# Layer 1's down projection as seven Strassen products in two passes, with the sums of weights and activations on GpSimd

## The chip, the cores and the metric

The kernel runs on one core of one Trainium2 chip. The metric is device microseconds (us) of one execution. The profile names the engines PE (TensorE matmul), PEld (TensorE weight load), DVE (VectorE), ACT (ScalarE), POOL (GpSimd) and SP (SyncE, which here only issues DMAs).

## The reference

A two-layer encoder trunk over 1024 tokens of 1024 channels, float32. The change concerns the feed-forward part, whose hidden width is 2816 = 22 x 128:

```python
def swiglu_ffn(h, w_gate, w_up, w_down):
    return (jax.nn.silu(h @ w_gate) * (h @ w_up)) @ w_down

for layer in range(2):
    h = rmsnorm(x, norm_mix_g[layer])
    x = x + mixer[layer](h)        # FNet and convolution heads in layer 0, pooling in layer 1
    h = rmsnorm(x, norm_ffn_g[layer])
    x = x + swiglu_ffn(h, ffn_w_gate[layer], ffn_w_up[layer], ffn_w_down[layer])
return rmsnorm(x, final_g)
```

## The kernel before

All activations lie transposed: 128 channels on the partitions, tokens along the free axis. Every float32 product is three matmuls of the reduced type fp32r, on operands split into a high and a low part: `mm3` issues high x high (L100), high x low (L101) and low x high (L102) into one PSUM bank. `split` makes the parts: a cast on ACT (L87), then a subtraction on DVE (L88).

**Gate and up.** Both matrices go through Winograd's form of Strassen's seven products. One step p covers two chunks of 128 hidden channels; the contraction is split into two halves of the channels (four chunks of 128 each) and the tokens into two halves of 512. `gate_up_first` does the two products that need only the first token half, for p = 0 to 10, and stores their sums in DRAM. `gate_up_all` then runs the other five, as 22 units (p, gate), (p, up): S2·T2, S3·T3, S1·T1, A22·T4, S4·B22, each 12 matmuls of 128x128 by 128x512. Two pairs share a bank: A22·T4 is accumulated on S3·T3's bank and S4·B22 on S1·T1's. So A22·T4 cannot start before DVE has read S3·T3 out of its bank (L668, `u3 = bd + u2`).

`prep` makes the left operands of the unit after the one in hand: two weight tiles `raw` (128x1024, issued by SP at L590) are loaded, DVE forms four sums from them (L634, L635, L636, L643), and five splits follow. `raw` has three buffers, the split weights ten. All engines work in order, so where such an instruction stands in its engine's queue decides what waits behind it. The products of gate and up, `g` (L652), leave by three DMAs for each p on POOL's queue (L653).

**Down.** `down` goes over the tokens in two parts (the second cut into blocks of 256 in its last stage) and over three groups of 8, 7 and 7 hidden chunks. Weights and activations are both loaded by SP into `raw` and split. Each result is added to x (L726). `final`, the last norm, runs over the last 256 tokens after the last product.

A tile scheduler places the instructions of each engine in its queue; reuse of a buffer waits for its last reader. `big` has 28 buffers (x, activations and the transformed activations), `half` six, `ln` four (`s3`, `u2`), `cvp` four (`g`), `cv` and `pr` two each.

Of the kernel before, what the change touches and what calls it, by code (L numbers as in the profile page):

```python
# [42 lines left out]
def trunk(ctx: ExitStack, tc: tile.TileContext, xT, vecs, cw, w_in, w_out, fmap, pmap,  # L43
          wg, wu, wd, cen_m, pcnt, dft_h, dft_l, seq_h, seq_l, out):
    nc = tc.nc
# [100 lines left out]

# [273 lines left out]
    for h in range(4):  # L420
        w = in_w(h)
        at = big("at")
        for t in range(2):
            TT(out=at[:, HALVES[t]], in0=in_mm(w, t), in1=invs[t], op=ALU.mult)
# [87 lines left out]

# [95 lines left out]
    def gate_up_first(layer, p, bt):  # L608
        """The products that need no more than the first half of the tokens."""
        g = half("g11")  # L610
        for i, wsrc in enumerate((wg, wu)):
# [10 lines left out]
            else:  # L622
                TT(out=g, in0=ps, in1=g, op=ALU.mult)
        nc.gpsimd.dma_start(a_dram[layer][2 * p][:, HALVES[0]], g)

    def prep(layer, p, wsrc, first):
        """Left operands of the products of one matrix, in the order of their use."""
        a11, a12 = raw_w(wsrc[layer, 2 * p])
        a21, a22 = raw_w(wsrc[layer, 2 * p + 1])
# [4 lines left out]
        TT(out=s3, in0=a11, in1=a21, op=ALU.subtract)  # L634
        TT(out=a21, in0=a21, in1=a22, op=ALU.add)  # L635
        TT(out=a11, in0=a21, in1=a11, op=ALU.subtract)  # L636
        w["S2"] = opnd(a11, wt)
        w["S3"] = opnd(s3, wt)
        w["S1"] = opnd(a21, wt)
        if first:  # L640
            w["A12"] = opnd(a12, wt)
        w["A22"] = opnd(a22, wt)
        TT(out=a12, in0=a12, in1=a11, op=ALU.subtract)  # L643
        w["S4"] = opnd(a12, wt)
        return w

    def fin(layer, up, dst, src, m, t, tmp=None):
        """dst becomes silu of the gate, then the product with up, which leaves."""
        if not up:
            nc.scalar.activation(dst, src, AF.Silu)  # L650
        else:
            TT(out=dst, in0=src, in1=dst, op=ALU.mult)  # L652
            nc.gpsimd.dma_start(a_dram[layer][m][:, HALVES[t]], dst)  # L653

# [116 lines left out]

# [18 lines left out]

# [81 lines left out]

# [3 lines left out]
    def final(pi, blocks):
        for lo, hi in blocks:
            inv = norm(lo, hi)
            yield 6.0
            for k in range(KD):  # L880
                o = half("o")[:, :hi - lo]
                STT(out=o, in0=xs[k][:, lo:hi], scalar=gneg[:, V_FIN + k:V_FIN + k + 1], in1=inv,
                    op0=ALU.mult, op1=ALU.mult)
                (nc.sync if k % 2 else nc.scalar).dma_start(out[k][:, lo:hi], o)
                yield 0.65
# [91 lines left out]
```

## Time and profile before

| | |
|---|---|
| time, median of 3 runs (range) | 1742.57 us (1741.8 to 1743.17) |
| span of the profiled execution | 1740.6 us, about 2 us under the median; the runs' times take in some 2 us around the span |
| granted TensorE clock, mean | 0.99 |
| gate and up of layer 0, 22 units of five products | about 454 to 754 us |
| gate and up of layer 1, the same | about 1181 to 1479 us |
| down of layer 1 | about 1479.7 to 1729.8 us |
| last norm after the last product | about 1729.8 to 1740.6 us |

In a row of a group the columns are: line, engine, operation, tiles out<-in, shapes, count | busy us, mean ns of one | idle time ahead and what ended it. In a row of the timeline: start, length, engine, line, operation, and in brackets the idle time before it and its releaser.

### The profile page before, as it was taken

To read this page: it belongs to the slowest core of one execution; us is meant where nothing else is said; L and a number is where in the kernel's file an instruction comes from. 1 tells how busy PE (TensorE), PEld (TensorE's weight loads), DVE (VectorE), ACT (ScalarE), POOL (GpSimd) and SP (SyncE) were. 2 spreads that over 40 slices of the span, in tenths; PEclk is the share of its full clock that TensorE was granted. 3 is DMA by queue.
4 is the path that set the end of the run, shared out by engine and by line. 5 is a ranking of instruction groups with operands and counts; after the bars stand their busy time and mean duration, and the time that the engine had idled before them with its cause. 6 is when DMAs were issued, how large, how long until landed. Compare 5 with 4: busy or idle time off the path is not lost.

```text
span 1740.6 us, 22375 instructions
## 1 busy us (share of the span) xinstructions
PE 1682.0 (97%) x8318; PEld 1400.9 (80%) x8318; DVE 1245.9 (72%) x1774; ACT 692.9 (40%) x1062; POOL 276.0 (16%) x300
## 2 busy tenths in 40 slices
PE   6998899999999999999999998999999999999997
PEld 4786777777888888889998886778888888788997
DVE  8699988794577777755559768787777775545546
ACT  5455855464323232233234344553232322334223
POOL 4587764111000000000000001110000000000000
PEclk9999899999999999999999999999999999999999
DMA  5121311545633333355433425646333333644433
GB/s 188 47 97 37 135 61 46 184 142 201 232 131 122 127 109 127 116 167 174 133 109 126 152 85 182 211 163 218 133 122 127 109 127 121 204 144 160 167 122 123
DMA packets 82236, 238.66 MB, mean 137 GB/s; under 512 B 10320, under 2 KB 15696, under 8 KB 82128
## 3 DMA queue, kind: packets, MB, share of 16 engines
q1 hardware_dynamic: 65520, 186.64, 32.6%
q0 software_dynamic: 14304, 47.46, 7.2%
q10 hardware_dynamic: 2304, 3.15, 0.5%
q8 instruction: 65, 1.06, 0.3%
q14 instruction: 43, 0.35, 0.1%
HBM read 190.02 MB, written 47.19 MB: 136 GB/s over the span
## 4 chain that ended last, share of the span: by engine, by line
PE 83%; DVE 11%; DMA 3%; ACT 1%; issue 1%; SPq 0%; DVEq 0%; ACTq 0%
PE ps L100 18%; PE ps L102 18%; PE ps L101 18%; PE lnp L100 10%; PE lnp L102 10%; PE lnp L101 9%; DVE acc L313 2%; DVE acc L134 1%; DMA xin<-in_xT 1%; DMA raw<-in_wd 1%; DVE hl L88 1%; DMA raw<-in_wu 1%; DVE wl L88 1%; DVE ybl L88 0%; PE lnp L538 0%
## 5 line engine op out<-in xcount | busy, mean ns | idle before, releaser
L87 ACT CAST hl<-raw 128x512 fp32r<-128x512 f32 x264 | 161.2, 621 | 426.0 <-DVE raw L636 161.4
L100 PE MATMUL ps<-hl 128*128 128x512 f32 x704 | 277.6, 395 | 3.3 <-ACT s L617 2.8
L102 PE MATMUL ps<-hl 128*128 128x512 f32 x704 | 276.6, 393 | 0.0
L101 PE MATMUL ps<-hl 128*128 128x512 f32 x704 | 276.5, 393 | 0.0
L87 ACT CAST wh<-raw 128x896 fp32r<-128x896 f32 (+2 forms) x139 | 132.5, 953 | 243.5 <-PE ps L101 109.0
L100 PE MATMUL ps<-ahl,wh 128*128 128x256 f32 (+3 forms) x711 | 228.0, 321 | 0.5 <-ACT wh L87 0.5
L102 PE MATMUL ps<-ahl,wl 128*128 128x256 f32 (+3 forms) x711 | 227.7, 320 | 0.5 <-DVE wl L88 0.5
L101 PE MATMUL ps<-ahl,wh 128*128 128x256 f32 (+3 forms) x711 | 227.2, 320 | 0.0
L88 DVE TENSOR_TENSOR hl<-raw,hl 128x512 fp32r<-128x512 f32 x264 | 179.8, 689 | 47.9 <-ACT hl L87 43.3
L100 PE MATMUL lnp<-hl 128*128 128x512 f32 x528 | 210.2, 398 | 0.7 <-ACT s L617 0.7
L102 PE MATMUL lnp<-hl 128*128 128x512 f32 x528 | 208.1, 395 | 0.0
L101 PE MATMUL lnp<-hl 128*128 128x512 f32 x528 | 207.9, 394 | 0.0
L88 DVE TENSOR_TENSOR wl<-raw,wh 128x896 fp32r<-128x896 f32 (+2 forms) x127 | 141.6, 1116 | 48.7 <-ACT wh L87 44.3
L100 PEld LDWEIGHTS ps<-hl 128*128 128x128 f32 x704 | 132.2, 188 | 37.7 <-ACT s L617 6.9
L102 PEld LDWEIGHTS ps<-hl 128*128 128x128 f32 x704 | 132.3, 188 | 30.6
L101 PEld LDWEIGHTS ps<-hl 128*128 128x128 f32 x704 | 132.4, 188 | 29.6
L303 POOL TENSOR_TENSOR cvp<-cvp,pr 128x512 f32<-128x512 f32 x96 | 139.3, 1452 | 82.5 <-ACT pr L302 78.2
L100 PEld LDWEIGHTS ps<-ahl,wh 128*128 128x128 f32 x711 | 134.3, 189 | 11.1 <-ACT wh L87 0.9
L102 PEld LDWEIGHTS ps<-ahl,wl 128*128 128x128 f32 x711 | 134.0, 189 | 10.9 <-DVE wl L88 1.0
L101 PEld LDWEIGHTS ps<-ahl,wh 128*128 128x128 f32 x711 | 134.3, 189 | 10.2 <-issue 0.2
L653 POOL DMA_DIRECT2D a<-g x66 | 35.6, 540 | 576.6 <-DVE g L652 576.6
L100 PEld LDWEIGHTS lnp<-hl 128*128 128x128 f32 x528 | 99.5, 189 | 27.3 <-ACT s L617 4.3
(209 smaller groups left out, 3095.9 us busy)
## 6 DMA issues: line engine op xcount, KB each, us to landing
raw<-in_wg SPq DMA_DIRECT2D x66, 512.0 KB, 3.4
raw<-in_wu SPq DMA_DIRECT2D x66, 512.0 KB, 3.6
raw<-in_wd SPq DMA_DIRECT2D x72, 448.0 KB, 3.3
a<-g POOLq DMA_DIRECT2D x88, 256.0 KB, 3.1
raw<-in_wd SPq DMA_DIRECT2D x32, 512.0 KB, 3.8
p<-s POOLq DMA_DIRECT2D x44, 256.0 KB, 3.2
u<-p SPq DMA_DIRECT2D x44, 256.0 KB, 4.2
raw<-a SPq DMA_DIRECT2D x44, 256.0 KB, 3.3
```

Source lines behind the costliest of these rows:

```text
L87: nc.scalar.copy(hi, src)
L88: (eng or nc.vector).tensor_tensor(out=lo, in0=src, in1=hi.bitcast(F32), op=ALU.subtract)
L100: nc.tensor.matmul(ps, lh, rh, start=start, stop=False, **kw)
L101: nc.tensor.matmul(ps, lh, rl, start=False, stop=False, **kw)
L102: mm = nc.tensor.matmul(ps, ll, rh, start=False, stop=stop, **kw)
L134: TT(out=acc, in0=acc, in1=sq, op=ALU.add)
L303: nc.gpsimd.tensor_tensor(out=a, in0=a, in1=pr, op=ALU.add)
L313: STT(out=acc, in0=src, scalar=wv, in1=acc, op0=ALU.mult, op1=ALU.add)
L653: nc.gpsimd.dma_start(a_dram[layer][m][:, HALVES[t]], dst)
```

## The change

Layer 1's down projection gets the same seven products, over pairs of hidden chunks and pairs of output chunks. For each p, its right operands are four blocks of g (B11, B21, B22, B12; two chunks by two token halves) and the sums T1 to T4. Pass A (`PASS_A`, five products: A11·B11, S2·T2, S3·T3, A12·B21, A22·T4) goes over p in blocks of 2, 3, 3, 3; pass B (S1·T1, S4·B22) in blocks of 4, 3, 4. A step is one block and one j, a pair of output chunks (four j). The left sums of a step come from two `raw` tiles of weights (`load_quads`, a new layout `wds`), the right operands from DRAM (`load_b`), loaded and split anew for each pass, for the block after the one in hand.

The T sums are made while gate and up run: after each (p, up) of layer 1, `combine` loads B11, forms four sums on POOL and stores them. The sums of `prep` move from DVE to POOL, in both layers. The last norm runs over 512 tokens instead of 256 after the last product. Layer 0's down keeps its old form.

Lines of the two kernels that belong together: 590/594 (weight load), 634, 635, 636, 643/638, 639, 640, 647 (sums), 652/656 (product with up), 653/664 (stores), 665/689, 668/692, 670/694, 677/701, 681/705 (reads of the banks), 88/89 (split).

```diff
+    PTT = nc.gpsimd.tensor_tensor
...
     def prep(layer, p, wsrc, first):
...
-        TT(out=s3, in0=a11, in1=a21, op=ALU.subtract)
-        TT(out=a21, in0=a21, in1=a22, op=ALU.add)
-        TT(out=a11, in0=a21, in1=a11, op=ALU.subtract)
+        PTT(out=s3, in0=a11, in1=a21, op=ALU.subtract)
+        PTT(out=a21, in0=a21, in1=a22, op=ALU.add)
+        PTT(out=a11, in0=a21, in1=a11, op=ALU.subtract)
         w["S2"] = opnd(a11, wt)
         w["S3"] = opnd(s3, wt)
         w["S1"] = opnd(a21, wt)
...
         w["A22"] = opnd(a22, wt)
-        TT(out=a12, in0=a12, in1=a11, op=ALU.subtract)
+        PTT(out=a12, in0=a12, in1=a11, op=ALU.subtract)
         w["S4"] = opnd(a12, wt)
...
+    def combine(p, g):
+        g11 = arena.tile([P, TH], F32, tag="cv", name="g11", bufs=2)
+        nc.sync.dma_start(g11, b_dram["B11"][p])
+        t1, t3 = g11, g["12"]
+        t2, t4 = (arena.tile([P, TH], F32, tag="pr", name=n, bufs=2) for n in ("t2", "t4"))
+        PTT(out=t1, in0=g["12"], in1=g11, op=ALU.subtract)
+        PTT(out=t2, in0=g["22"], in1=t1, op=ALU.subtract)
+        PTT(out=t3, in0=g["22"], in1=g["12"], op=ALU.subtract)
+        PTT(out=t4, in0=g["21"], in1=t2, op=ALU.subtract)
+        for name, src in (("T1", t1), ("T2", t2), ("T3", t3), ("T4", t4)):
+            store_b(1, name, p, src)
...
             gate_up_rest(layer, p, bt, w, up, p >= nfirst, g)
+            if up and layer == 1:
+                combine(p, g)
             w = nxt
...
+    def left_a(j, p0, n):
+        a11, a12, a21, a22 = load_quads(j, p0, n)
+        w = {"A11": wopnd(a11)}
+        s3 = small("s3")[:, :n * P]
+        PTT(out=s3, in0=a11, in1=a21, op=ALU.subtract)
+        PTT(out=a21, in0=a21, in1=a22, op=ALU.add)
+        PTT(out=a21, in0=a21, in1=a11, op=ALU.subtract)
+        w["S2"], w["S3"], w["A12"], w["A22"] = wopnd(a21), wopnd(s3), wopnd(a12), wopnd(a22)
+        return w
+
+    def left_b(j, p0, n):
+        a11, a12, a21, a22 = load_quads(j, p0, n)
+        PTT(out=a21, in0=a21, in1=a22, op=ALU.add)
+        PTT(out=a11, in0=a21, in1=a11, op=ALU.subtract)
+        PTT(out=a12, in0=a12, in1=a11, op=ALU.subtract)
+        return {"S1": wopnd(a21), "S4": wopnd(a12)}
...
+    def down_strassen(layer, blocks_a, blocks_b, gen):
+        steps = [("a", p0, n, j) for p0, n in blocks_a for j in range(4)]
+        steps += [("b", p0, n, j) for p0, n in blocks_b for j in range(4)]
...
+        for i, (kind, p0, n, j) in enumerate(steps):
+            if j == 0 and i + 4 < len(steps):
+                todo, got = right_names(i + 4)[1], []
+            nw = left(i + 1) if i + 1 < len(steps) else None
+            if kind == "a":
+                ba, bb, bd = single(), single(), single()
+                product(ba, w["A11"], b["B11"], True, True)
+                u = half("u1")
+                nc.scalar.copy(u, ba)
+                product(bb, w["S2"], b["T2"], True, True)
...
+                    PTT(out=u2[j], in0=u2[j], in1=u, op=ALU.add)
+                    TT(out=u2[j], in0=bb, in1=u2[j], op=ALU.add)
+                product(bd, w["S3"], b["T3"], True, True)
+                TT(out=x22, in0=bd, in1=x22, op=ALU.add)
+                product(ba, w["A12"], b["B21"], False, True)
+                TT(out=x11, in0=ba, in1=x11, op=ALU.add)
+                product(bd, w["A22"], b["T4"], False, True)
+                TT(out=x21, in0=bd, in1=x21, op=ALU.add)
...
+            k = -(-len(todo) // (4 - j) // 2) * 2
+            got += load_b(todo[:k])
...
-    down(1, ([(0, TH)], [(TH, TH + 256), (TH + 256, S)]), final)
+    down_strassen(1, ((0, 2), (2, 3), (5, 3), (8, 3)), ((0, 4), (4, 3), (7, 4)), final)
```

How the queues change at three places. The number behind a tile's name tells one buffer's use from another.

POOL in layer 1's gate and up, steps p = 2 and 3, before: only the stores of g.

```order
L653 DMA a1_5_2332<-g22_10102 128x512
L653 DMA a1_5_2332<-g21_10103 128x512
L653 DMA a1_4_2331<-g12_10104 128x512
L653 DMA a1_7_2334<-g22_10304 128x512
L653 DMA a1_7_2334<-g21_10305 128x512
L653 DMA a1_6_2333<-g12_10306 128x512
```

And now, from the third T sum of p = 2. `raw_10468`, `raw_10470` are the weights of (4, gate), `raw_10581`, `raw_10583` those of (4, up).

```order
L674 TENSOR_TENSOR g12_10181<-g22_10179,g12_10181 128x512
L675 TENSOR_TENSOR t4_10359<-g21_10180,t2_10358 128x512
L664 DMA bT1_2_2362<-g11_10356 128x512
L664 DMA bT2_2_2373<-t2_10358 128x512
L664 DMA bT3_2_2384<-g12_10181 128x512
L664 DMA bT4_2_2395<-t4_10359 128x512
L639 TENSOR_TENSOR raw_10470<-raw_10470 128x512
L640 TENSOR_TENSOR raw_10468<-raw_10470,raw_10468 128x512
L647 TENSOR_TENSOR raw_10468<-raw_10468 128x512
L638 TENSOR_TENSOR s3_10585<-raw_10581,raw_10583 128x512
L639 TENSOR_TENSOR raw_10583<-raw_10583 128x512
L640 TENSOR_TENSOR raw_10581<-raw_10583,raw_10581 128x512
```

The sums of weights now stand on POOL behind the T sums of p = 2 and their four stores.

DVE in the unit (3, up), before, from the last split of the unit ahead:

```order
L88 TENSOR_TENSOR hl_10401<-raw_10380,hl_10401 128x512
L634 TENSOR_TENSOR s3_10486<-raw_10482,raw_10484 128x512
L635 TENSOR_TENSOR raw_10484<-raw_10484 128x512
L665 TENSOR_TENSOR u2_10407<-ps_10404,u2_10407 128x512
L636 TENSOR_TENSOR raw_10482<-raw_10484,raw_10482 128x512
L643 TENSOR_TENSOR raw_10482<-raw_10482 128x512
L88 TENSOR_TENSOR hl_10490<-raw_10482,hl_10490 128x512
L668 TENSOR_TENSOR u3_10434<-lnp_10406,u2_10407 128x512
```

And now the same place:

```order
L89 TENSOR_TENSOR hl_10489<-raw_10468,hl_10489 128x512
L689 TENSOR_TENSOR u2_10495<-ps_10492,u2_10495 128x512
L89 TENSOR_TENSOR hl_10589<-raw_10581,hl_10589 128x512
L692 TENSOR_TENSOR u3_10522<-lnp_10494,u2_10495 128x512
L89 TENSOR_TENSOR hl_10592<-s3_10585,hl_10592 128x512
L694 TENSOR_TENSOR u3_10522<-lnp_10493,u3_10522 128x512
```

The four sums are gone from DVE, and the split of S2 of (4, up), which reads the last POOL row shown, stands ahead of the read L692 of (3, up), as it stood ahead of L668.

SP in the down, before: weights and activations in turn.

```order
L110 DMA raw_12758<-in_wd 128x1024
L110 DMA raw_12847<-in_wd 128x1024
L711 DMA raw_12905<-a1_8_2335 128x512
L110 DMA raw_12910<-in_wd 128x1024
L711 DMA raw_12974<-a1_9_2336 128x512
L110 DMA raw_12979<-in_wd 128x1024
```

And now, around the last step of the block of p = 5 to 7 in pass A. `bT2`, `bT3` with numbers 8 to 10 are right operands of the next block; `raw_13024`, `raw_13026` are the weights of the last step of the block in hand.

```order
L804 DMA raw_13006<-bT2_9_2380 128x512
L804 DMA raw_13006<-bT2_10_2381 128x512
L804 DMA raw_13015<-bT3_8_2390 128x512
L804 DMA raw_13015<-bT3_9_2391 128x512
L815 DMA raw_13024<-in_wds 128x2x384
L815 DMA raw_13026<-in_wds 128x2x384
```

Between two weight tiles now stand two tiles of right operands, and `raw_13026` takes the buffer of `raw_13006`, whose second half is cast into a `big` tile that the step's own first product reads last.

More of the change, by code (lines that the diff above doesn't have):

```diff
@@ L43, in trunk @@
 def trunk(ctx: ExitStack, tc: tile.TileContext, xT, vecs, cw, w_in, w_out, fmap, pmap,
-          wg, wu, wd, cen_m, pcnt, dft_h, dft_l, seq_h, seq_l, out):
+          wg, wu, wd, wds, cen_m, pcnt, dft_h, dft_l, seq_h, seq_l, out):
     nc = tc.nc
@@ L527, in single @@
         return bank(("ps", "lnp", "ps")[turn[0] % 3])
-    a_dram = [[dram.tile([P, S], F32, name=f"a{layer}_{f}") for f in range(NF)] for layer in range(2)]
+    a_dram = [[dram.tile([P, S], F32, name=f"a0_{f}") for f in range(NF)]]
+    b_dram = {n: [dram.tile([P, TH], F32, name=f"b{n}_{p}") for p in range(NF // 2)]
+              for n in ("B11", "B21", "B22", "T1", "T2", "T3", "T4")}
     def norm(lo, hi):
@@ L548, in product @@
     def product(ps, w, b, start, stop):
-        for j in range(4):
+        n = len(b)
+        for j in range(n):
             c = j * P
             mm3(ps, (w[:, c:c + P], w[:, TH + c:TH + c + P]), (b[j][:, :TH], b[j][:, TH:]),
-                start and j == 0, stop and j == 3, skip_group_check=not start)
+                start and j == 0, stop and j == n - 1, skip_group_check=not start)
     def h_make(layer, t, bt, hf):
@@ L623, in gate_up_first @@
                 TT(out=g, in0=ps, in1=g, op=ALU.mult)
-        nc.gpsimd.dma_start(a_dram[layer][2 * p][:, HALVES[0]], g)
+        store_b(layer, "B11", p, g)
     def prep(layer, p, wsrc, first):
@@ L770, in down, with load_b, load_quads @@
         run_behind(back, 1e9)
+    def load_b(names):
+        out = []
+        for i in range(0, len(names), 2):
+            raw = arena.tile([P, 1024], F32, tag="raw", name="raw", bufs=3)
+            for j, (n, p) in enumerate(names[i:i + 2]):
+                nc.sync.dma_start(raw[:, j * TH:(j + 1) * TH], b_dram[n][p])
+            for j in range(len(names[i:i + 2])):
+                out.append(opnd(raw[:, j * TH:(j + 1) * TH], big))
+        return out
+    def load_quads(j, p0, n):
+        out = []
+        for q in range(2):
+            raw = arena.tile([P, 1024], F32, tag="raw", name="raw", bufs=3)
+            rv = raw.rearrange("p (a c) -> p a c", a=2)[:, :, :n * P]
+            nc.sync.dma_start(rv, wds[j, :, 2 * q:2 * q + 2, p0 * P:(p0 + n) * P])
+            out += [raw[:, :n * P], raw[:, TH:TH + n * P]]
+        return out
@@ new lines, in wopnd @@
+    def wopnd(src):
+        t = wtile("hl")
+        n = src.shape[-1]
+        split(t[:, :n], t[:, TH:TH + n], src)
+        return t
+    PASS_A = (("A11", "B11"), ("S2", "T2"), ("S3", "T3"), ("A12", "B21"), ("A22", "T4"))
+    def left_a(j, p0, n):
[7 more added lines that the diff above has]
+        return w
@@ new lines, in left_b, with right_names, right, left @@
+    def left_b(j, p0, n):
[7 more added lines that the diff above has]
+        steps += [("b", p0, n, j) for p0, n in blocks_b for j in range(4)]
+        def right_names(i):
+            kind, p0, n, j = steps[i]
+            rights = [b for _, b in PASS_A] if kind == "a" else ["T1", "B22"]
+            return rights, [(b, p) for b in rights for p in range(p0, p0 + n)]
+        def right(i, got):
+            rights, names = right_names(i)
+            n = steps[i][2]
+            return {b: got[k * n:(k + 1) * n] for k, b in enumerate(rights)}
+        def left(i):
+            kind, p0, n, j = steps[i]
+            return (left_a if kind == "a" else left_b)(j, p0, n)
+        w = left(0)
+        b = right(0, load_b(right_names(0)[1]))
+        for k in range(KD):
+            xs[k] = big(f"x{k}")
+            nc.sync.dma_start(xs[k], x_dram[layer][k])
+        x = [[[xs[2 * j + r][:, hs] for hs in HALVES] for r in range(2)] for j in range(4)]
+        u2 = [None] * 4
+        back, budget = [None], 0.0
+        todo, got, late = [], [], None
+        def finish_b(bc, s4, b22, x12):
+            product(bc, s4, b22, False, True)
+            TT(out=x12, in0=bc, in1=x12, op=ALU.add)
+        for i, (kind, p0, n, j) in enumerate(steps):
+            if j == 0 and i + 4 < len(steps):
+                todo, got = right_names(i + 4)[1], []
+            nw = left(i + 1) if i + 1 < len(steps) else None
+            (x11, x12), (x21, x22) = x[j]
+            if kind == "a":
[4 more added lines that the diff above has]
+                product(bb, w["S2"], b["T2"], True, True)
+                if u2[j] is None:
+                    u2[j] = arena.tile([P, TH], F32, tag="cvp", name="uu", bufs=4)
+                    TT(out=u2[j], in0=bb, in1=u, op=ALU.add)
+                else:
+                    PTT(out=u2[j], in0=u2[j], in1=u, op=ALU.add)
[6 more added lines that the diff above has]
+                TT(out=x21, in0=bd, in1=x21, op=ALU.add)
+                if (p0, n) == blocks_a[-1]:
+                    TT(out=x21, in0=x21, in1=u2[j], op=ALU.add)
+                    for dst in (x12, x22):
+                        PTT(out=dst, in0=dst, in1=u2[j], op=ALU.add)
+            else:
+                bc = single()
+                product(bc, w["S1"], b["T1"], True, True)
+                TT(out=x22, in0=bc, in1=x22, op=ALU.add)
+                if late:
+                    finish_b(*late)
+                late = bc, w["S4"], b["B22"], x12
+            budget = run_behind(back, budget + 0.3 * n * (5 if kind == "a" else 2))
+            k = -(-len(todo) // (4 - j) // 2) * 2
+            got += load_b(todo[:k])
+            todo = todo[k:]
+            if j == 3:
+                if (p0, n) == blocks_a[-1] and kind == "a":
+                    back, budget = [gen(0)], 0.0
+                if i + 1 < len(steps):
+                    b = right(i + 1, got)
+            w = nw
+        finish_b(*late)
+        run_behind(back, 1e9)
+        for _ in gen(1):
+            pass
@@ L874, in trunk, with final @@
     gate_up_all(1, b1, NP1)
[L876 to L885, printed above, removed]
-    down(1, ([(0, TH)], [(TH, TH + 256), (TH + 256, S)]), final)
+    def final(t):
+        hs = HALVES[t]
+        inv = norm(hs.start, hs.stop)
+        yield 6.0
+        for k in range(KD):
+            o = half("o")
+            STT(out=o, in0=xs[k][:, hs], scalar=gneg[:, V_FIN + k:V_FIN + k + 1], in1=inv,
+                op0=ALU.mult, op1=ALU.mult)
+            (nc.sync if k % 2 else nc.scalar).dma_start(out[k][:, hs], o)
+            yield 0.65
+    down_strassen(1, ((0, 2), (2, 3), (5, 3), (8, 3)), ((0, 4), (4, 3), (7, 4)), final)
 def _round_f32r(a):
@@ L947 @@
     wd = []
-    for l in range(2):
+    for l in range(1):
         parts, o = [], 0
@@ L954 @@
     a["wd"] = np.stack(wd)
+    a["wds"] = np.ascontiguousarray(
+        f["ffn_w_down"][1].reshape(NF // 2, 2, P, 4, 2, P).transpose(3, 2, 4, 1, 0, 5)).reshape(4, P, 4, NF // 2 * P)
     a["cen"] = (np.eye(P) - 1.0 / P).astype(np.float32)
```

8 lines of the change are left out of this document (7 added, 1 removed).

## The prediction

> **What bounds the kernel now.** I read the page's busy shares and the chain that ended last, then a table of windows over the stages, then the timeline of one unit.
>
> ```profile
> span 1740.6 us, 22375 instructions
> PE 1682.0 (97%) x8318; PEld 1400.9 (80%) x8318; DVE 1245.9 (72%) x1774; ACT 692.9 (40%) x1062; POOL 276.0 (16%) x300
> POOL 4587764111000000000000001110000000000000
> PE 83%; DVE 11%; DMA 3%; ACT 1%; issue 1%; SPq 0%; DVEq 0%; ACTq 0%
> ```
>
> PE is the bound, and POOL is idle in the stages at hand. The windows (us, then busy us with counts of PE, PEld, DVE, ACT, POOL, then granted clock, DMA share, GB/s) are gate and up of layer 0, of layer 1, the down of layer 1, the tail:
>
> ```profile
> 454.00:754.00 300.00, 299.76 (x1296) 243.06 (x1296) 211.40 (x322) 86.05 (x140) 17.81 (x33) 1.00 0.39 134
> 1182.60:1478.90 296.30, 296.02 (x1284) 240.43 (x1282) 214.56 (x328) 86.40 (x142) 16.88 (x32) 1.00 0.38 131
> 1479.70:1729.90 250.20, 249.39 (x1588) 225.42 (x1588) 142.26 (x208) 86.57 (x118) 0.54 (x1) 1.00 0.48 156
> 1729.90:1740.60 10.70, 0.70 (x2) 0.30 (x2) 5.41 (x13) 0.89 (x2) 0.00 (x0) 0.73 0.29 98
> ```
>
> PE runs without a hole and at full clock in all three. So fewer matmuls are a gain in full, DVE's relief is worth nothing by itself, and every new wait of PE is a loss in full. How much room the waits have is seen in one unit of layer 1, (p, gate), which begins at 1257.56:
>
> ```profile
> 1243.71 0.40 PE L100 MATMUL ps<-hl 128*128 128x512 f32 x1
> 1246.48 0.39 PE L100 MATMUL lnp<-hl 128*128 128x512 f32 x1
> 1256.40 0.33 SPq L590 DMA_DIRECT2D raw<-in_wg  x1
> 1259.67 0.69 DVE L634 TENSOR_TENSOR s<-raw 128x512 f32<-128x512 f32 x1
> 1260.39 0.69 DVE L635 TENSOR_TENSOR raw<-raw 128x512 f32<-128x512 f32 x1
> 1261.60 0.68 DVE L636 TENSOR_TENSOR raw<-raw 128x512 f32<-128x512 f32 x1
> 1263.10 0.69 DVE L88 TENSOR_TENSOR hl<-raw,hl 128x512 fp32r<-128x512 f32 x1
> 1263.71 0.68 DVE L668 TENSOR_TENSOR g<-ps,u 128x512 f32<-128x512 f32 x1
> 1260.05 0.54 POOL L653 DMA_DIRECT2D a<-g  x1 [2.25 <-DVE g L652]
> ```
>
> A product takes 1246.48 - 1243.71 = 2.77 us, a matmul 0.231, a unit of five 13.85, a step p 27.7. The weights land 3.3 us after their issue (1256.40 to L634 at 1259.67). The chain is load, sums, split of S2, then L668, since L668 stands behind that split. It ends at 1264.39; the A22 product of this unit starts three products in, at 1257.56 + 8.3 = 1265.86. So there are 1.5 us of slack. The last g of a step reaches its store 2.5 us after the step's last product (1260.05 against 1257.56).
>
> **The price of a sum on POOL, and its quarrel with DVE.**
>
> ```profile
> L303 POOL TENSOR_TENSOR cvp<-cvp,pr 128x512 f32<-128x512 f32 x96 | 139.3, 1452 | 82.5 <-ACT pr L302 78.2
> L88 DVE TENSOR_TENSOR hl<-raw,hl 128x512 fp32r<-128x512 f32 x264 | 179.8, 689 | 47.9 <-ACT hl L87 43.3
> L87 ACT CAST hl<-raw 128x512 fp32r<-128x512 f32 x264 | 161.2, 621 | 426.0 <-DVE raw L636 161.4
> L653 POOL DMA_DIRECT2D a<-g x66 | 35.6, 540 | 576.6 <-DVE g L652 576.6
> raw<-in_wg SPq DMA_DIRECT2D x66, 512.0 KB, 3.4
> L303 POOL TENSOR_TENSOR cvp<-cvp,pr x96: 1272/1300/2861, 58.8 to 276.8; 128x512 f32<-128x512 f32 x96
> 119.15 14.06 POOL L303 TENSOR_TENSOR cvp<-cvp,pr 128x512 f32<-128x512 f32 x9
> 127.52 0.68 DVE L424 TENSOR_TENSOR at<-ps,v 128x512 f32<-128x512 f32 x1
> 129.11 1.52 DVE L433 TENSOR_TENSOR zs<-at 128x256 f32<-128x256 f32 x1
> 131.99 1.50 DVE L435 TENSOR_TENSOR at<-at 128x256 f32<-128x256 f32 x1
> 133.41 0.41 DVE L436 TENSOR_TENSOR at<-zs 128x256 f32<-128x256 f32 x1
> ```
>
> The same sum is 0.69 us on DVE. On POOL it is 1.30 as the median (the second row on L303 has shortest, median, longest in ns), 1.45 as the mean, 1.56 as nine in 14.06 us. I take 1.30 where a sum waits for no other, 1.38 where it reads the one before, since the mean holds the waits told of next; 1.27 and 1.56 are the ends. While those nine ran (to 133.21), DVE instructions with two SBUF operands took 1.5 us; the next one took 0.41, and one that read PSUM took its 0.68. So either such a DVE instruction or POOL's sum waits for the other, up to a whole sum; in a chain I count 0.5 us for each meeting. The Trainium skill, SBUF — State Buffer, section "Who interferes with whom", says that an exclusive lock stands between a DVE instruction reading two SBUF inputs and a GpSimd one; the 1.5 against 0.41 us agrees, and without it some twenty meetings, one a step in either layer, or 10 us, would fall away.
>
> **The parts.**
>
> *Fewer products.* Down of layer 1 has 22 x 8 x 2 x 3 = 1056 matmuls of 512 columns, and will have 11 x 4 x 7 x 3 = 924. 132 x 0.231 = 30.5 us; the blocks of 256 at the old end add 0.8. **-31.3 us.** This is sure.
>
> *Sums of weights on POOL, layer 0.* Chain of a gate unit: three sums (L638, L639, L640) 3 x (1.38 - 0.69) = 2.1 longer, one meeting 0.5, engine changes 0.3; less the 1.5 of slack: 1.4 us of waiting at A22 a step. In the up unit DVE is rid of two instructions of the old chain that stood between the sums and the split, L665 and L643 (0.69 each), so that I count nothing there. 1.4 a step over 11 steps: **+15 us**, ends 0 and 25 (the same relief in the gate unit; the wait in both units, for which the stores of g, 0.54 each and ahead on POOL's queue, speak).
>
> *Layer 1: sums, T sums and stores in one POOL queue.* Let a step's last product end at 0. T1 needs the last g, at 2.5. Then T1, one s3 and three T sums, 5 x 1.30: 9.0. Four stores of 0.54: 11.2. L639, L640 of (4, gate): 13.9. Casts and splits of that unit follow (S2, S3, S1, a silu between, L701, A22; 4.7 us by 0.62 and 0.69): 18.6. Only the A22 split frees the buffer of (4, up)'s second weight tile: loaded at 22.0 (3.4 by the row on in_wg). Three sums: 26.1; cast 0.62 and S2's subtraction 0.69, one meeting 0.5: 27.9. L692 stands behind that: 28.6. PE wants the bank at 13.85 + 8.3 = 22.1. So PE stands **6.5 us in every (p, up)**, and a later end of this step starts the next chain later by as much: nothing is recovered. Nine steps (p = 0 and the last have no such chain behind them): **+58 us**, ends 15 and 95. The low end is a chain some 5 us shorter a step (POOL's stores behind its sums); the high end has POOL at 1.56 and a meeting at each split.
>
> *The clock after each stall.* Two idle stretches of PE in the first 300 us, and those right behind them (us, PE busy, clock, DMA share, GB/s):
>
> ```profile
> 168.20:176.20 8.00, 0.03 (x1) 0.70 0.00 0
> 176.20:181.70 5.50, 5.40 (x20) 0.50 0.00 0
> 284.20:287.30 3.10, 0.79 (x4) 1.00 0.26 69
> 287.50:290.90 3.40, 3.40 (x7) 0.50 0.16 66
> ```
>
> After an idle stretch of 2.3 us or more PE ran at half clock for 3.4 to 5.5 us, which loses 1.7 to 2.75. At 1.9 a stall, nine times: **+17 us**, ends 0 and 25. The Trainium skill, TensorE: Matmul & The Clock Gate, Part 1, tells of a half rate after idleness in windows of about 3.4 us; the 3.40 us row agrees.
>
> *Down, pass A.* Rights are loaded anew, 11 x 5 tiles, each 0.62 on ACT and 0.69 on DVE; lefts at 384 columns about 1.05 on POOL (0.75 x 1.38), 0.55 on DVE. A step of three p is 45 matmuls, 10.4 us of PE; POOL 3 x 1.05 + 1.38 = 4.5, DVE about 9. So no engine is the bound, but the three `raw` buffers take four tiles a step, against one for each 2.77 us now, each held for 3.4 us of landing plus sums and splits, 6 to 10 in all: 4/3 x 6 to 10 = 8 to 13 us a step against 10.4. I take a loss of 1 for most of 16 steps: +14, ends 0 and 25. At the block ends there is more: `big` has 28 buffers, x takes 8 and two blocks of rights 30. So next-block rights (`raw_13006`) wait for the first product of the last step, and `raw_13026`, that step's own weights, for them: cast and subtraction 1.5 after that product's first third (0.7), landing 3.4, three sums 3.2, split of S2 1.0: 9.8, where PE wants S2 at 2.1. Nearly 8 us and 2 of half clock, at two block ends: +20, ends 5 and 30. **Together +34 us.**
>
> *Down, pass B.* Two products a step: 5.5 us of PE at four p, 4.15 at three. The loop through `raw` is landing 3.4, two to three sums of 1.38 (1.05), one split 1.3: about 7 and 6. 8 x 1.5 + 4 x 1.9 is 20; I take **+18 us**, ends 5 and 40.
>
> *The tail.* From the last product to the end:
>
> ```profile
> 1729.79 0.42 DVE L726 TENSOR_TENSOR x<-lnp,x 128x256 f32<-128x256 f32 x1 [1.14 <-PE lnp L102]
> 1733.92 2.07 DVE L882 SCALAR_TENSOR_TENSOR o<-x,gneg,v 128x256 f32<-128x256 f32 x5
> 1736.34 1.33 DVE L882 SCALAR_TENSOR_TENSOR o<-x,gneg,v 128x256 f32<-128x256 f32 x3 [0.36 <-DMA out<-o]
> ```
>
> Some 13 DVE instructions of 0.42 become 0.69 to 0.74 (+4), the casts and the norm's matmul and the stores grow by half a us each: **+5.5 us**, ends 3 and 8.
>
> Sum: -31.3 + 15 + 58 + 17 + 34 + 18 + 5.5 = +116. 1740.6 + 116 = 1857; with the 2 us by which the median of the runs stands over this span, **1859 us**.
>
> **The rivals.**
>
> 1. *The slack holds, and the product count decides* (faster). If POOL's T sums came out early enough (the stores after the sums cost nothing, the splits never meet POOL), the chain of 28.6 would have to shrink by 6.5 to PE's 22.1: that is the point from which layer 1 is free. Then -31.3, the tail +5.5 and 5 of small waits: 1722. For it: DVE has 28% of slack in layer 1 and POOL would be busy 12 x 1.38 of 27.7 us only. Against: the wait is one of order, not of load.
> 2. *Layer 1's gate and up holds, the down does not*: -31.3 + 10 + 34 + 18 + 5.5 = +36, and a third of layer 1's 75: 1804. For it: DVE's queue and the buffers are as I followed them by hand, a meeting or a landing less takes off a third each.
> 3. *Worse than summed*: every meeting with DVE costs a full sum, layer 0 +25, layer 1 +95 and +25, down +80, the tail +8: about 1945. For it are the 1.5 us rows; against, the 0.68 us row: ten of 23 DVE instructions a step read PSUM.
> 4. *Cold clock rule off*: with waits of 6 us that leave the clock alone, 17 less, 1842. That lies in my own range.
>
> **How the numbers follow.** My case (with the fourth) has 0.62, from 1820 to 1900; rival 2 has 0.20; rival 3 has 0.10; rival 1 has 0.06, and 0.02 for a balance by chance. What a measurement here can tell from no change is 0.2%, 3.5 us. So slower 0.92, same 0.02, faster 0.06. The range leaves out rival 1 and most of rival 3, and takes in rival 2: 1775 to 1915.
>
> **What would show it.** Right: in layer 1's up units PE stands some 6 us ahead of the A22 product with L692 as its releaser, a step takes 34 to 36 us instead of 27.7, and the granted clock is under 1 there; L89 on DVE shows rows of over 1 us; PE's busy time in down falls by some 31 us, yet the stage is longer than 250 us, with two holes of about 8 us in pass A and steps of 6 to 7 us in pass B; the tail is 16 us. Wrong: no hole at L692 (POOL's T sums come early, or the weights' buffer is freed by an earlier reader), or a stage of down close to 220 us.

## The result, and the profile after

The changed kernel takes 1918.07 us (median of 4 runs, 1916.23 to 1921.45) against 1742.87 before: ratio 1.1006, 95% interval 1.0988 to 1.1023. It is slower by 175 us, where 116 were forecast with a range up to 1915. The page's first lines and the chain:

```profile
span 1919.7 us, 21791 instructions
PE 1706.4 (89%) x7656; PEld 1367.8 (71%) x7656; DVE 1211.0 (63%) x1681; ACT 703.6 (37%) x1150; POOL 703.0 (37%) x657
PE 24%; POOL 16%; issue 14%; DMA 10%; DVE 8%; ACT 3%; POOLq 0%; SPq 0%; DVEq 0%; ACTq 0%
```

PE is busy for 89% of the span instead of 97, DVE for 63 and POOL for 37: the path is handed round. PE's share of the chain fell from 83 to 24% and POOL's rose to 16%. The windows by stage, columns as before: gate and up of layer 0; the stretch to layer 1's units; gate and up of layer 1; pass A; pass B; the tail.

```profile
468.30:803.60 335.30, 311.33 (x1311) 246.30 (x1309) 173.79 (x251) 86.34 (x142) 121.04 (x112) 0.99 0.36 120
803.60:1220.70 417.10, 404.07 (x2228) 348.08 (x2229) 291.35 (x432) 173.22 (x273) 37.41 (x59) 0.99 0.45 149
1220.70:1600.80 380.10, 325.95 (x1315) 260.01 (x1314) 177.33 (x261) 85.48 (x153) 190.79 (x187) 0.92 0.39 132
1600.80:1809.00 208.20, 167.08 (x662) 127.01 (x661) 128.48 (x200) 74.73 (x149) 86.82 (x77) 0.93 0.45 147
1809.00:1902.90 93.90, 71.95 (x260) 50.00 (x259) 59.03 (x80) 25.28 (x45) 39.18 (x31) 0.93 0.51 157
1902.90:1919.70 16.80, 1.91 (x4) 0.30 (x3) 10.02 (x15) 1.84 (x3) 0.00 (x0) 0.62 0.34 125
```

A stage is bounded here, in every kernel, by the first read of a bank in a layer's units, the last one, and the start of the last matmul of the last product; these are the stages' lengths in us.

| | front | layer 0 gate, up | between | layer 1 gate, up | down | tail | span |
|---|---|---|---|---|---|---|---|
| before | 466.5 | 302.4 | 413.0 | 299.1 | 248.6 | 11.1 | 1740.6 |
| after | 468.3 | 335.3 | 417.1 | 380.1 | 302.2 | 16.7 | 1919.7 |
| difference | +1.8 | +32.9 | +4.1 | +81.0 | +53.6 | +5.6 | +179.1 |
| forecast | 0 | +15 | 0 | +75 | +20.7 | +5.5 | +116 |

What PE waited for (total us, times, longest), in layer 0's units, in layer 1's, in the down (there L897 reads S3·T3's bank in pass A, and L909 S1·T1's in pass B):

```profile
PE ps L101 <- DVE g L692: 15.7, 10, 3.3
PE lnp L101 <- DVE u L692: 5.2, 7, 1.0
PE lnp L101 <- ACT hl L88: 2.3, 3, 0.8
...
PE lnp L101 <- DVE u L692: 51.6, 10, 5.8
...
PE ps L101 <- ACT hl L88: 24.4, 14, 7.2
PE lnp L101 <- DVE x L897: 18.3, 9, 6.3
PE ps L101 <- DVE x L909: 6.9, 5, 2.0
```

In layer 1 it is one wait, ten times, nine of them nearly 6 us, and its releaser is L692, as forecast. The chain behind one of them, on POOL, SP, ACT, DVE and PE:

```profile
1321.25 1.29 POOL L672 TENSOR_TENSOR g<-g,g 128x512 f32<-128x512 f32 x1 [2.33 <-DVE g L656]
1327.48 0.56 POOL L664 DMA_DIRECT2D bT<-g  x1
1329.65 1.31 POOL L639 TENSOR_TENSOR raw<-raw 128x512 f32<-128x512 f32 x1
1336.73 0.33 SPq L594 DMA_DIRECT2D raw<-in_wu  x1
1340.23 1.29 POOL L638 TENSOR_TENSOR s<-raw 128x512 f32<-128x512 f32 x1 [6.53 <-DMA raw<-in_wu]
1344.22 0.62 ACT L88 CAST hl<-raw 128x512 fp32r<-128x512 f32 x1 [6.30 <-POOL raw L640]
1344.88 1.21 DVE L89 TENSOR_TENSOR hl<-raw,hl 128x512 fp32r<-128x512 f32 x1 [6.32 <-ACT hl L88]
1346.01 0.68 DVE L692 TENSOR_TENSOR u<-lnp,u 128x512 f32<-128x512 f32 x1
1346.83 0.77 PE L101 MATMUL lnp<-hl 128*128 128x512 f32 x1 [5.55 <-DVE u L692]
```

The step ended at 1318.94, where PE starts the next unit. From there: T1 at 2.3 us (forecast 2.5), weights issued at 17.8 (18.6), landed at 21.3 (22.0), cast at 25.3 (26.1), L692 done at 27.8 (28.6). Note that POOL is idle for 6.5 us inside this chain, waiting for a load. The split of S2 takes 1.21 us where the next rows' take 0.68: it runs beside POOL's L647.

The clock around that stall (us, PE busy, clock, DMA share, GB/s):

```profile
1340.90:1346.80 5.90, 0.38 (x2) 0.75 0.19 67
1346.90:1350.40 3.50, 3.50 (x9) 0.50 0.00 0
1350.50:1360.00 9.50, 9.50 (x42) 0.99 0.53 194
```

At half clock the matmuls start 0.43 us apart instead of 0.23, so 3.5 us of it cost some 1.6 us. Behind five of the nine long holes it lasted 3.5 to 3.9 us, behind the four others 5.7 to 6.1. Adding up, over PE's rows in a stage, what the distance of two matmuls has above 0.2305 (differences of 0.02 to 0.25 us as slow clock, larger ones as holes) gives for layer 1 17.5 us of clock and 59.3 of holes, for pass A 9.8 and 45.8, for pass B 5.8 and 28.5.

### The profile page after: what moved, and what is told of

Its sections match the earlier page's. It is cut to its first block, busy times and chain, and to the rows that moved or that the text cites. A ratio compares the mean times of both kernels' runs of the same rounds, so it can differ in the third digit from the quotient of the medians.

```text
span 1919.7 us, 21791 instructions
## 1 busy us (share of the span) xinstructions
PE 1706.4 (89%) x7656; PEld 1367.8 (71%) x7656; DVE 1211.0 (63%) x1681; ACT 703.6 (37%) x1150; POOL 703.0 (37%) x657
## 4 chain that ended last, share of the span: by engine, by line
PE 24%; POOL 16%; issue 14%; DMA 10%; DVE 8%; ACT 3%; POOLq 0%; SPq 0%; DVEq 0%; ACTq 0%
PE ps L101 5%; PE ps L102 4%; PE ps L103 4%; DMA raw<-in_wds 4%; DVE hl L89 4%; PE lnp L101 4%; PE lnp L103 3%; PE lnp L102 3%; POOL raw L639 3%; POOL raw L640 3%; DMA raw<-in_wu 3%; POOL s L638 2%; ACT hl L88 2%; POOL bT L664 1%; POOL raw L647 1%
## 5 line engine op out<-in xcount | busy, mean ns | idle before, releaser
L89 DVE TENSOR_TENSOR hl<-raw,hl 128x512 fp32r<-128x512 f32 (+2 forms) x429 | 321.4, 762 | 334.8 <-ACT hl L88 331.0
L88 ACT CAST hl<-raw 128x512 fp32r<-128x512 f32 (+2 forms) x429 | 247.7, 596 | 755.2 <-POOL raw L640 312.9
L101 PE MATMUL ps<-hl 128*128 128x512 f32 x894 | 360.0, 403 | 60.0 <-ACT hl L88 24.4
L103 PE MATMUL ps<-hl 128*128 128x512 f32 x894 | 355.9, 399 | 2.7 <-DVE hl L89 2.7
L102 PE MATMUL ps<-hl 128*128 128x512 f32 x894 | 356.3, 399 | 0.0
L101 PE MATMUL lnp<-hl 128*128 128x512 f32 x646 | 271.3, 420 | 88.4 <-DVE u L692 56.8
L102 PE MATMUL lnp<-hl 128*128 128x512 f32 x646 | 264.3, 409 | 0.0
L103 PE MATMUL lnp<-hl 128*128 128x512 f32 x646 | 263.2, 408 | 0.6 <-DVE hl L89 0.5
L101 PEld LDWEIGHTS ps<-hl 128*128 128x128 f32 x894 | 170.3, 191 | 116.5 <-ACT hl L88 46.9
L101 PEld LDWEIGHTS lnp<-hl 128*128 128x128 f32 x646 | 127.9, 198 | 137.2 <-ACT hl L88 69.0
L103 PEld LDWEIGHTS ps<-hl 128*128 128x128 f32 x894 | 170.5, 191 | 46.2 <-DVE hl L89 6.5
L102 PEld LDWEIGHTS ps<-hl 128*128 128x128 f32 x894 | 170.8, 191 | 38.0 <-issue 0.5
L103 PEld LDWEIGHTS lnp<-hl 128*128 128x128 f32 x646 | 127.6, 198 | 32.5 <-DVE hl L89 2.1
L102 PEld LDWEIGHTS lnp<-hl 128*128 128x128 f32 x646 | 128.1, 198 | 28.5 <-issue 1.0
L638 POOL TENSOR_TENSOR s<-raw 128x512 f32<-128x512 f32 x44 | 59.4, 1351 | 176.0 <-DMA raw<-in_wu 169.5
L88 ACT CAST wh<-raw 128x1024 fp32r<-128x1024 f32 (+2 forms) x83 | 78.0, 939 | 119.9 <-DMA raw<-in_wd 43.4
L101 PE MATMUL ps<-ahl,wh 128*128 128x504 f32 (+2 forms) x358 | 115.2, 322 | 0.0
L103 PE MATMUL ps<-ahl,wl 128*128 128x504 f32 (+2 forms) x358 | 114.8, 321 | 0.0
L102 PE MATMUL ps<-ahl,wh 128*128 128x504 f32 (+2 forms) x358 | 114.7, 320 | 0.0
L89 DVE TENSOR_TENSOR wl<-raw,wh 128x896 fp32r<-128x896 f32 (+2 forms) x71 | 78.3, 1105 | 28.3 <-ACT wh L88 25.4
```

The source lines that it names most:

```text
L88: nc.scalar.copy(hi, src)
L89: (eng or nc.vector).tensor_tensor(out=lo, in0=src, in1=hi.bitcast(F32), op=ALU.subtract)
L101: nc.tensor.matmul(ps, lh, rh, start=start, stop=False, **kw)
L102: nc.tensor.matmul(ps, lh, rl, start=False, stop=False, **kw)
L103: mm = nc.tensor.matmul(ps, ll, rh, start=False, stop=stop, **kw)
L638: PTT(out=s3, in0=a11, in1=a21, op=ALU.subtract)
```

## The experiments

All are the changed kernel with one edit, if nothing else is said. The new medians stand against 1918 us.

**Sums of weights back on DVE.**

```diff
     def prep(...):          # the same in all four sums
-        PTT(out=s3, in0=a11, in1=a21, op=ALU.subtract)
+        TT(out=s3, in0=a11, in1=a21, op=ALU.subtract)
```

> The four sums of weights of gate and up go back to DVE; the T sums, their stores and the down projection stay as changed. Theory (queue order): PE waits at the A22 product because the read of its bank stands on DVE behind a split that waits for POOL's queue. Then the waits of layer 0 (32 us) and of the stage ahead of layer 1's units (about 10) go, and of layer 1's 77 us at most 8 stay: about 1804 us. Rival (the port): POOL's T sums alone keep DVE's subtractions back, in every step of layer 1: 20 to 40 us stay there, 1825 to 1845 us.

Measured 1831.99 us. Layer 0 is at 302.9 us and the stretch behind it at 411.1, as before: all of their loss is POOL's sums. But layer 1 keeps 30 us (329.7), so the first theory was too short, and the rival's number is met. DVE, then POOL, in one step of that kernel:

```profile
1297.41 1.70 DVE L638 TENSOR_TENSOR s<-raw 128x512 f32<-128x512 f32 x1 [0.22 <-DMA raw<-in_wg]
1299.15 1.67 DVE L639 TENSOR_TENSOR raw<-raw 128x512 f32<-128x512 f32 x1
1300.74 0.68 DVE L689 TENSOR_TENSOR u<-ps,u 128x512 f32<-128x512 f32 x1
1301.34 1.18 DVE L640 TENSOR_TENSOR raw<-raw 128x512 f32<-128x512 f32 x1
1302.55 1.67 DVE L647 TENSOR_TENSOR raw<-raw 128x512 f32<-128x512 f32 x1
...
1304.75 0.68 DVE L692 TENSOR_TENSOR g<-ps,u 128x512 f32<-128x512 f32 x1
...
1298.64 1.63 POOL L673 TENSOR_TENSOR t<-g,g 128x512 f32<-128x512 f32 x1
1300.23 1.74 POOL L674 TENSOR_TENSOR g<-g,g 128x512 f32<-128x512 f32 x1
```

DVE's sums and POOL's take turns: three of DVE's four are 1.7 us long instead of 0.69 (the other 1.18), POOL's 1.6 to 1.7 instead of 1.29, while L689, which reads PSUM, keeps its 0.68. The Trainium skill, SBUF — State Buffer, "Who interferes with whom", has this as an exclusive lock on a shared read port, not met by a DVE instruction with one SBUF input; the trace agrees on both.

**All sums of the units on DVE.** The edit above, and in `combine`:

```diff
-        PTT(out=t1, in0=g["12"], in1=g11, op=ALU.subtract)     # all four
+        TT(out=t1, in0=g["12"], in1=g11, op=ALU.subtract)
```

> Both the sums of weights of gate and up and the T sums are on DVE; POOL keeps the stores, and the down projection's own sums. Theory (the port): what was left in layer 1 with the weights' sums alone on DVE, 30 us, came from POOL's T sums and DVE's sums holding each other up (1.7 us each in place of 0.69 and 1.3); without a POOL sum in the stage it goes: about 1802 us. Rival (queue order): T sums that wait for the last g and for B11 stand on DVE ahead of reads of banks: 10 to 25 us stay, 1812 to 1827 us.

Measured 1809.97 us; layer 1 at 301.2. So the 30 us go with POOL's T sums. In the step shown above the chain from the start of L638 to the end of L692 takes 8.0 us; the same chain took 4.7 in the unit that the prediction read, with 1.5 us of slack. That leaves a wait of 1.8, and PE waits 2.1 us there in eight steps: the turns at the port explain it. What is left over 1743 is the tail and the down, which at 310.4 is 8 us longer than in the changed kernel: PE waits 5.5 us at the start of pass A, for a cast that the changed kernel has in time. Why it comes later was not tried.

**T sums on DVE, sums of weights on POOL.** The edit in `combine` alone.

> The T sums of layer 1 are made on DVE; the sums of weights stay on POOL. Theory (queue order): POOL's queue loses four sums a step (5.2 us) but keeps the stores; the wait in a step of layer 1 falls from 6.1 to the 2.8 of layer 0, and no stall is long enough for the half clock: 77 falls to about 32, so about 1873 us. Rival: DVE's T sums wait for the last g and for B11, and the reads of the banks stand behind them: the wait stays, about 1915 us.

Measured 1873.43 us, layer 1 at 327.1, 28 us over the kernel before: a step then costs about what it costs in layer 0. The down is at 310.5, as with all sums on DVE.

**T stores from ACT's queue.**

```diff
-            store_b(1, name, p, src)                      # in combine
+            nc.scalar.dma_start(b_dram[name][p], src)
```

> The four stores of the T sums of a step go through ACT's DMA queue instead of POOL's. Theory (queue order): the chain loses 4 x 0.54 = 2.2 us a step, over nine steps 19 us, the half clock stays: about 1899 us. Rival: ACT's queue waits for POOL's last T sum with four issues, its casts come later by as much, and nothing or less than nothing is won: 1918 to 1930 us.

Measured 1899.39 us, layer 1 at 360.7, 19.4 less: the four issues on POOL's queue count in full.

**Reads first in gate and up.**

```diff
     # gate_up_rest; splits of the next unit are emitted here, not in prep
-        TT(out=u3, in0=bc, in1=u3, op=ALU.add)
+        read = TT(out=u3, in0=bc, in1=u3, op=ALU.add)
+        if mid:
+            mid(read)                     # the next unit's splits
     # in splits, for S2 and S3
+            lo = TT(out=t[:, TH:], in0=src, in1=t[:, :TH].bitcast(F32), op=ALU.subtract)
+            tc.add_manual_dep(lo.ins, read.ins.name, ..., reason="read first")
```

> Only the order on DVE is changed, in both layers' gate and up: the splits of S2 and S3 of the next unit stand behind the reads of S3T3's and S1T1's banks (L692, L694) instead of ahead of them; every sum stays on POOL. Theory (queue order): the split has half a unit of room behind these reads, so the waits at A22 go in both layers: -32 and -70, about 1815 us. Rival (load of POOL, the port): the chain through POOL sets the pace of a step itself, or the splits then come too late for the next unit; the wait moves to the first product of a unit and at most 30 us are won, 1890 us or more.

Measured 1866.84 us. Layer 0 is at 304.0, its waits gone; layer 1 at 355.1, with waits of 2.7 to 3.6 us at the same read left in seven steps, since the last split of the unit before (S4's) still stands ahead of the reads and waits for POOL's fourth sum. So in layer 0 the order on DVE decides; in layer 1 only part of it was moved.

**The kernel before, with the four sums on POOL.**

```diff
-        TT(out=s3, in0=a11, in1=a21, op=ALU.subtract)             # all four of prep
+        nc.gpsimd.tensor_tensor(out=s3, in0=a11, in1=a21, op=ALU.subtract)
```

> The kernel before, with the four sums of weights of gate and up on POOL and nothing else changed. Theory: the same 33 us in each layer's gate and up as in layer 0 of the changed kernel, and some 5 where units and the first products overlap: about 1813 us. Rival (the waits of layer 0 come from elsewhere in the changed program): under 1765 us.

Measured 1805.72 us: layer 0 331.0, layer 1 329.2, down and tail untouched. The layers pay 29 and 30 us for these four lines alone.

**Left sums of the down on DVE.**

```diff
-        PTT(out=a21, in0=a21, in1=a22, op=ALU.add)      # all sums of left_a and left_b
+        TT(out=a21, in0=a21, in1=a22, op=ALU.add)
```

> The sums of the down projection's left operands are made on DVE, all else as changed. Theory (the loop load, sums, splits through three buffers sets the pace of a step of the down): three sums are 1.6 us shorter a step and meet no POOL sum, of 28 steps about 1.2 us each are won: about 1885 us. Rival (DVE's queue sets it): 1.65 us more on DVE a step stand ahead of the reads of the banks, nothing is won: 1910 to 1925 us.

Measured 1901.21 us, 17 of the 33 us expected; the down takes 281.3 instead of 302.2. PE's waits for L897 fell from 18.3 to 10.0 us, those for casts from 24.4 to 17.8. So the loop with POOL in it is part of the loss, and not all.

**Smaller blocks in pass A.**

```diff
-    down_strassen(1, ((0, 2), (2, 3), (5, 3), (8, 3)), ...)
+    down_strassen(1, ((0, 2), (2, 2), (4, 2), (6, 2), (8, 3)), ...)
```

> Pass A's blocks are 2, 2, 2, 2, 3 in place of 2, 3, 3, 3: x (8 tiles) and two blocks of rights (10 each) fit into the 28 big buffers. Theory: the two waits of 7.6 us at the block ends and their half clock go; 16 steps of two p at 9.4 us and 4 of three at 11.5 make 196 us in place of 210: about 1904 us. Rival (the weight buffers alone make those waits): they stay at every block end, now four, and four more steps are paid: 1925 to 1940 us.

Measured 1920.37 us, the down 303.2. In the changed kernel the hole at a block end is this (PE, then SP, POOL and ACT):

```profile
1674.89 0.39 PE L103 MATMUL ps<-hl 128*128 128x512 f32 x1
1682.49 0.80 PE L101 MATMUL ps<-hl 128*128 128x512 f32 x1 [7.21 <-ACT hl L88]
...
1664.89 10.82 SPq L815 DMA_DIRECT2D raw<-in_wds  x2
1678.76 0.99 POOL L831 TENSOR_TENSOR s<-raw 128x384 f32<-128x384 f32 x1 [0.99 <-DMA raw<-in_wds]
1681.93 0.51 ACT L88 CAST hl<-raw 128x384 fp32r<-128x384 f32 x1 [5.51 <-POOL raw L833]
```

The second weight load is issued at the end of those 10.82 us, at about 1675.4; PE waits for it, the sums and the cast.

With the smaller blocks PE waits for casts 7.4 us in all, against 24.4, so these holes did go; but its waits for L897 rose from 18.3 to 33.2. The gain was given back within the stage, so neither side held: the rival had the holes stay.

```profile
PE lnp L101 <- DVE x L897: 33.2, 17, 7.1
PE ps L101 <- ACT hl L88: 7.4, 8, 1.9
```

**Reads first in the down.**

```diff
-                TT(out=x22, in0=bd, in1=x22, op=ALU.add)             # pass A; in pass B with bc
+                splits(TT(out=x22, in0=bd, in1=x22, op=ALU.add))     # the next step's, each made to depend on it
```

> Only the order on DVE in the down is changed: the splits of the next step's left operands stand behind the read of S3T3's bank (L897, pass A) or of S1T1's (L909, pass B). Theory (queue order): PE's waits for these reads, some 32 us, go: about 1886 us. Rival (the loop through the buffers): the splits then come that much later, and PE waits for them at the next step's products; at most 8 us are won: 1910 us or more.

Measured 1921.9 us, the down 304.1: the rival held. PE's waits for the read that was L897 fell from 18.3 to 10.5 us, those for casts rose from 27.9 to 33.2, and the stage became no shorter. Order alone was not the bound here.

**One more raw buffer.**

```diff
-        raw = arena.tile([P, 1024], F32, tag="raw", name="raw", bufs=3)
+        raw = arena.tile([P, 1024], F32, tag="raw", name="raw", bufs=4)
-        return arena.tile([P, WW], dt, tag="big", name=name, bufs=28)[:, :cols]
+        return arena.tile([P, WW], dt, tag="big", name=name, bufs=27)[:, :cols]
```

> One more buffer for raw tiles (4 in place of 3), one less of the big ones (27 in place of 28), all else as changed. Theory (each loop load, POOL sums, splits is closed by the release of a raw buffer): in a step of layer 1 the weights of (4, up) are loaded before the A22 split of (4, gate), their sums follow L647 at 15 us after the step's end, S2 is split at 21 and L692 meets PE's 22.1: layer 1 falls by 60 to 75 us, layer 0 by 25 to 30, the down by 30: about 1785 us. Rival (POOL's queue or DVE's order alone closes them): less than 30 us in all, 1890 us or more.

Measured 1773.94 us: 144 us won with every sum still on POOL. Layer 0's units, layer 1's, and the down:

```profile
458.70:763.20 304.50, 304.50 (x1319) 246.48 (x1319) 196.81 (x252) 91.11 (x145) 128.03 (x108) 1.00 0.42 133
1176.00:1480.60 304.60, 302.95 (x1309) 245.54 (x1308) 217.78 (x261) 92.25 (x152) 213.49 (x187) 1.00 0.51 167
1480.60:1756.10 275.50, 234.79 (x926) 180.14 (x925) 192.20 (x278) 99.83 (x194) 128.86 (x106) 0.93 0.50 160
```

POOL is busy for 213 of 305 us in layer 1 and PE hardly waits, at clock 1.00. So POOL's load and its turns with DVE do not stop PE by themselves. They lengthen the loop of load, sums and splits, which the release of one of three buffers closes; with a fourth the units are as long as in the kernel before with four (304.9 and 304.2, next run).

**The kernel before with that buffer**, as the control.

> The kernel before with four raw buffers and 27 big ones. Its gate and up and its down have no holes to win, but the first 460 us do, where the changed kernel with the buffer gained 9 us: about 1734 us. Then the combined kernel (1736 us) wins nothing by the change itself. Rival: the 9 us came from the changed program: 1743 us.

Measured 1734.04 us (ratio 0.9943, 0.9924 to 0.9963). The front is at 460.5 and the stretch between at 406.4, 12.6 less together; the units, at 304.9 and 304.2, give back 7.6 of it by these bounds, and the down is at 246.6.

**Buffer, and left sums on DVE.** Sums of weights and T sums stay on POOL.

> As changed, with four raw buffers, 27 big ones and the left sums of the down on DVE; sums of weights and T sums stay on POOL. Theory (the down's rest is POOL's sums in the loop, and the port): the down falls from 275 to some 250 us: about 1748 us. Rival (the order of reads and splits on DVE): it stays over 268 us, 1765 us or more.

Measured 1745.45 us, the down 244.5: what held the down at 275 with four buffers was POOL's part in it. PE's longest wait in pass A is then 2.0 us, so the block-end holes are gone too, with the same blocks and one big buffer less.

**Combined:** the edits of `prep`, `combine`, `left_a` and `left_b`, four raw buffers and 27 big ones, and in pass A:

```diff
+                product(bd, w["S3"], b["T3"], True, True)
+                TT(out=x22, in0=bd, in1=x22, op=ALU.add)
                 product(bb, w["S2"], b["T2"], True, True)
...
-                product(bd, w["S3"], b["T3"], True, True)
-                TT(out=x22, in0=bd, in1=x22, op=ALU.add)
```

> All sums of gate and up, the T sums and the left sums of the down on DVE; four raw buffers, 27 big ones; in pass A the product S3T3 ahead of S2T2, so that the read of its bank has two products of time. If the gains add up: 1810 - 21 (left sums) - 30 (buffer) - 8 (order): about 1751 us, no faster than before; if the down's loop goes wholly, 1720 us; if DVE becomes the bound there, 1780 us.

Measured 1736.16 us (0.9959, 0.9943 to 0.9975), the down 245.6.

**Combined, with pass A in blocks of 2, 2, 2, 2, 3.**

> As the combined kernel, with pass A in blocks of 2, 2, 2, 2, 3. With the loop through the buffers eased, the two block ends (7.5 us and half clock each) are worth what they cost: 15 us under the combined kernel, about 1736 us. Rival: the more frequent steps still pay more than that, as with three buffers: equal or slower.

Measured 1743.04 us: 7 slower than the combined kernel, the down 251.2. Here the rival held.

**Combined, with reads first instead of the exchanged products.**

> The combined kernel, with the splits of the next step's left operands behind the reads of S3T3's and S1T1's banks in place of the exchanged products. If order on DVE is what is left in the down (245 us against 213 of products), it falls to 235: about 1726 us. Rival: the splits come too late for the next step: 1736 us or more.

Measured 1736.91 us, the down 245.1: no gain over the combined kernel.

**Combined, five raw buffers, 26 big ones.**

> The combined kernel with five raw buffers and 26 big ones. If the loop through the raw buffers still holds the down, its waits (32 us) halve: about 1720 us. Rival (DVE, 215 of 246 us busy there, and the big buffers at the block ends): less than 4 us are won, 1732 to 1740 us.

Measured 1725.56 us (0.9885, 0.9866 to 0.9905), the best of all kernels here: the down is at 237.6, of which products at full clock are 924 x 0.2305 = 213. It lies between theory and rival: of the 32 us that the combined kernel's down had over its products 8 went, a quarter, and most of the other gain is in the units. That is 8.5 us under the kernel before with four buffers; the kernel before with five was not run, so what of it the change itself is worth stays open.

```profile
1470.20:1707.80 237.60, 222.30 (x926) 175.41 (x924) 217.54 (x360) 101.18 (x194) 33.25 (x24) 0.98 0.58 187
```

## Why the prediction was wrong

The direction, the place of the largest loss and its mechanism were right; the time missed the range by 3 us, because two terms were too small by 51 us together, layer 1 by 6, and another 6 ahead of the units were left out.

- *Fewer products.* Right. At 0.2305 us the 924 matmuls are 213 us of the down.
- *Layer 1's queue on POOL*, forecast +58 and +17 for the clock, measured +81 in all, by the trace 59.3 of holes and 17.5 of clock. Each link of the chain came within 0.9 us. Part of the fit is luck: the nine holes of the chain are 5.8 us each where 6.5 were forecast, 53 together, and small holes that were not counted make up the rest; and the 1.9 us of clock a stall is right only as the mean of two kinds of stall. The release of the buffer, which that chain had as one link ("Only the A22 split frees the buffer"), turned out to be enough by itself: a fourth buffer takes the stall away with all the rest left in place. The forecast did not draw that conclusion from its own chain. What the stores cost (19 us) and the T sums (with the port) was shown one by one.
- *Layer 0*, forecast +15, measured +32.9. This term failed. The gate unit's 1.4 us is right (15.7 us over ten units). The step that failed is "so that I count nothing there": the up unit waits too, up to 1 us for L692 or a cast, 7.5 us in all; with the other small holes of the stage that is 27 us, and 4.2 of slow clock, of which none was counted. The kernel before with only these sums on POOL shows the same 29 us a layer.
- *Ahead of the units*, counted at nothing: +5.9 us. It goes with the sums of weights back on DVE (411.1 us for the stretch between). By the waits there, PE stood up to 5 us for a copy on ACT (L621) that lay behind casts of the first units' operands, which waited for POOL.
- *Down*, forecast a loss of 34 + 18 = 52 us over its products, measured 302.2 - 213.0 = 89. This term failed most. The block ends are right in place and size (7.2 us of waiting, twice, and half clock behind it). The step that failed is "I take a loss of 1 for most of 16 steps": with its block ends pass A lost 56 us instead of 34. In nine of its 16 steps PE waited at the read L897 (18.3 us, among them one hole of 6.3 and one of 3.2 in the last block), and in eight others places for splits (6.7 us beside the block ends); pass B lost 34 instead of 18, and stalls on half clock cost 15.6 us in the two passes where 4 were counted. Taking the loop of each buffer at its mean, without the waiting of one queue on another, was too kind; its high ends (25, 30 and 40) together would have held it. That the loop is what was sized too small shows in the runs: a fourth buffer takes 27 us off the down, left sums on DVE 21, both together 58.
- *The tail*, forecast +5.5, measured +5.6.
- *Rivals.* That the clock would stay (the fourth) is out: 0.50 behind each long stall. The first rival, that the slack holds, has its point in one buffer: with four, both layers' units run as fast as before within 2%. The third had the losses of layer 0 and of the down nearly in size (25 and 80, measured 33 and 89), and put far too much on layer 1 (120, measured 81).

## What to carry to other kernels

Before work moves to a slower engine, follow the loop that it stands in (load, sum, split, release of the buffer) and compare the loop's length with the time that the buffers in rotation give; where it just fits, an idle engine is no room, and one more buffer can be worth more than any choice of engine. Put the read that frees a PSUM bank ahead of work that waits for loads, but look first whether that work is itself the bound, for then the wait only moves. And let a control have the same buffer: the Strassen form saves 30 us of products, yet with four buffers in both it came out level with the old form (1736 and 1734); a fifth put it 8.5 us ahead of the old form with four, which is not yet a comparison of the two forms.

## What was not expected of the hardware

That DVE and POOL sums slow each other in full turns (1.67 and 1.7 us against 0.69 and 1.29) was known from 256-column rows of the kernel before; that it would cost 30 us in layer 1 with four POOL sums a step, and no more than 3 with four buffers and all twelve sums a step on POOL (304.6 against the 301.6 of the combined kernel, and 304.2 in the kernel before with four), was not: beside slack the same meetings are nearly free. Half clock after a hole of about 6 us did not last equally long: 3.5 to 3.9 us five times and 5.7 to 6.1 four times, 17.5 us lost in all. Nor does the length of a hole settle whether it comes: with the sums of weights back on DVE, layer 1 has eight holes of the same 2.1 us, and behind three of them PE ran at half clock for 3.5 to 4.0 us, behind the other five at full clock.
